# Samples' x and small vectors on SyncE's queue, the next columns' first weight steps inside the opening's list, and that list in another order

## The chip, the cores and the metric

The kernel runs on one core of a Trainium2 chip. A core has five engines with a queue of instructions each, which run side by side and wait for one another through semaphores: TensorE (PE, matmuls; its weight loads are shown apart as PEld), VectorE (DVE), ScalarE (ACT), GpSimd (POOL) and SyncE (SP, which here only issues DMAs). ACT and POOL can issue DMAs too. Such an issue takes its place in the engine's queue: what stands behind it waits until it has been issued. The metric is the time of one execution in microseconds (us); less is better.

## The reference

One step of a decoder layer, with a prompt of 1024 rows and 8 samples of 8 rows (1088 rows in all), 1024 columns wide:

```
shift, scale, gate = silu(c) @ w_ada + b_ada
h = rmsnorm(x, norm_g) * (1 + scale) + shift
u_pool | z_pool | z_ssm | xBC | dt | g = h @ w_in
p = (pool_mix(u_pool) * silu(z_pool)) @ w_pool_out
s = rmsnorm((SSD(silu(conv(xBC))) + D*x) * silu(z_ssm)) @ w_ssm_out
x = x + gate * ((sigmoid(g_pool) * p + sigmoid(g_ssm) * s) @ w_o);   y = rmsnorm(x, final_g)
```

c has one row for the prompt and one for each sample, so that the modulation (shift, scale, gate) is a table of 9 rows. The states of pooling, convolution and SSD are outputs too.

## The kernel before

Everything is f32; a matmul operand is cut into a high part (rounded to the fast format, by ACT) and a low part (the rest, by DVE or POOL), and a product is three matmuls: high by high, low by high, high by low. The big projection h @ w_in is done two columns of 128 at a time, with one level of Strassen (seven half-size products for eight): a "pair". A pair loads its two columns into two tiles named rawA (three buffers in all), whose halves are b11, b21, b12, b22; from them come t3 = b22 - b12, t2 = t3 + b11, t4 = t2 - b21 and b12 - b11 (line 368), and each of the seven is split (lines 153 and 156). On the other side stand sums of parts of h, kept as S1 to S4.

The kernel has an opening (function first, lines 641 to 1087), then a long stage of pairs (products at line 414), the SSD and the output products. The change touches the opening and what follows it at once.

The opening does its work by a list, ORDER1 (line 611): each word is a small function for one or a few instructions, and each engine, SP among them, runs its part of the words in the order of the list (in_line). A letter behind a word says the engine: V for DVE, A for ACT, G for POOL. The words:

- sq (line 667 on DVE, 669 on ACT) squares a tile of x and sums it. Tiles 0 to 7 are the prompt's, 128 rows each; tile 8 is the samples'. root, unit, spread and rsb (lines 673 to 703) turn the sums of a group of tiles into a row factor, spread over the partitions. The groups are tiles 0 and 1, 2 to 4, and 5 to 8.
- turn (709) transposes one column block k of one group on PE; out (714) multiplies it by the row factor into tf.
- silu, tab, cturn, sct (718 to 729) prepare c; vturn, vt (732 to 736) the small vectors vb. ada (759) multiplies c by one eighth of a quarter of w_ada; mr, end, md (764 to 779) turn a quarter's result into columns and add the biases. So md0 to md3 give shift and scale for two column blocks each.
- h, ta, t, l (790 to 812) apply the modulation and split h. hi, lo, pr (825 to 842) are the split and the products of the first two gate columns, sg their sigmoid (853).
- dt, dto, gt, ge (864 to 884) make dt and the gate's table; ge also stores the table (884). lx, lt, lc are the late small vectors.
- ca, cb, cc, ce (918 to 927) are the Strassen sums of h, s1h to s4h and s1l to s4l (931, 933 and 654) their splits; tc, tb, d21, d12, wh, wl (line 825 and 654) the weights of the opening's own pair, m (982) its products, u and z (998 to 1010, 991) what is made of them.
- warm runs matmuls of ones.

A word that subtracts or adds on DVE or POOL does so in a helper at line 654, so many rows have that line.

DMAs of the opening: ACT issues c (lines 133, 134), the samples' x (139) and four small loads into vb (141 to 144), ahead of all its other work. SP works through a list `waiting`, each entry as soon as the words it names have been said:

```
for what in ("x07", "p0", "w", "p1", "p2"):
waiting += [((), lambda: w_load(0, 1)), (("lo0.0",), lambda: w_load(1, 1))]
waiting += [(("ada1.6",), lambda k=k: ada_load(3, k)) for k in range(KT)]
waiting += [((), lambda: dtw.append(dt_w()))]
waiting += [(("end1",) + tuple(f"sq{i}" for i in range(9)), lambda: col(0)), (("end2",), lambda: col(1))]
waiting += [((), lambda: late.append(late_loads())), ((), bg_load)]
waiting += [(tuple(f"turn2.{k}" for k in range(KT)), lambda k=k: gate_load(k)) for k in range(KT)]
```

That is eight tiles of x, the first quarter of w_ada, the first halves of two gate columns, two quarters of w_ada, the other halves, the last quarter, dt's weights, the opening's own two columns (948), the late small vectors (251 to 255), the gate's bias (1028) and the gate's third of w_ada (609).

The pairs after the opening are run by run_units, which fetches the weights of a pair (pair_w, line 351) one unit ahead: it loads the columns, splits b11, and leaves the other steps in a generator (steps), of which the pair before does some between its products and the pair itself the rest. The first of these pairs (columns 2 and 3 of z) is built after the opening; but its instructions aren't in the list, and the scheduler of the program may put them between the list's instructions where it thinks an engine free.

## Time and profile before

| | us |
|---|---|
| median of 3 runs (1271.11 to 1277.57) | 1273.59 |
| profiled execution, as it was timed | 1276.04 |
| its span in the profile | 1274.3 |
| PE busy in the span | 1245.2 (98%) |
| DVE, ACT, POOL busy | 976.5, 682.1, 729.6 |
| first product of the pair after the opening starts | 106.32 |

A row of a timeline has the start and the length in us, the engine, the line, the operation, what it writes and reads, the shapes, how many instructions are put together in it, and in brackets how long the engine had been idle and what ended that. Rows of an engine with a q (ACTq, SPq) are DMA issues: their time is that of the issue, not of the transfer. A row of busy time by stretch has its columns told where it is shown.

### The profile page before, as it was taken

How to read it: one execution, taken by the hardware profiler on the slowest of the kernel's cores; microseconds unless marked ns; L12 is line 12 of the kernel's file. 1: busy time of each engine (PE TensorE's matmuls, PEld its weight loads, DVE VectorE, ACT ScalarE, POOL GpSimd, SP SyncE). 2: the span in 40 equal slices, each digit the busy share in tenths (PEclk: the TensorE clock that was granted, in tenths of full speed). 3: DMA queues.
4: the chain of work that ended last, by engine and by line, in shares of the span. 5: the costliest groups of instructions: out<-in, count | busy, mean ns of one | idle time of the engine just before them, and what ended most of it. 6: DMA issues, size and time to landing. Idle time of an engine off the chain costs nothing.

```text
span 1274.3 us, 26561 instructions
## 1 busy us (share of the span) xinstructions
PE 1245.2 (98%) x9733; PEld 1163.7 (91%) x9733; DVE 976.5 (77%) x1709; ACT 682.1 (54%) x1568; POOL 729.6 (57%) x617
## 2 busy tenths in 40 slices
...
GB/s 323 297 97 192 139 156 153 183 190 158 166 162 196 162 154 169 139 147 120 184 167 196 162 182 155 318 314 269 249 237 282 272 256 244 276 214 222 248 194 154
DMA packets 264676, 258.00 MB, mean 202 GB/s; under 512 B 29889, under 2 KB 204561, under 8 KB 264538
## 3 DMA queue, kind: packets, MB, share of 16 engines
...
## 4 chain that ended last, share of the span: by engine, by line
PE 86%; DVE 4%; DMA 4%; ACT 3%; issue 2%; POOL 1%; SPq 1%; ACTq 0%; POOLq 0%; DVEq 0%
PE ps L414 22%; PE mm L414 22%; PE mm L239 16%; PE pc L414 5%; PE ps L1256 2%; PE pc L1578 2%; PE ps L2060 2%; PE ps L2062 2%; PE ps L2061 2%; PE ps L1259 2%; DMA R<-in_w_o 1%; PE ps L1346 1%; PE ps L1553 1%; PE ps L982 1%; DMA wo<-R 1%
## 5 line engine op out<-in xcount | busy, mean ns | idle before, releaser
L156 POOL TENSOR_TENSOR wlo<-rawA,whi 128x512 fp32r<-128x512 f32 x120 | 174.7, 1460 | 110.6 <-ACT whi L153 98.5
L156 POOL TENSOR_TENSOR wlo<-raw,whi 128x512 fp32r<-128x512 f32 x90 | 149.2, 1665 | 86.3 <-ACT whi L153 74.3
L239 PE MATMUL mm<-Y,whi 128*128 128x352 f32 (+1 forms) x960 | 197.5, 336 | 0.5 <-ACT G L1787 0.3
L239 PEld LDWEIGHTS mm<-Y,whi 128*128 128x128 f32 x960 | 160.4, 190 | 7.1 <-issue 4.8
L1099 DVE SCALAR_TENSOR_TENSOR GA<-GA,cvT,GA 128x1112 f32<-128x1112 f32 x72 | 131.2, 1826 | 0.1
L414 PE MATMUL mm<-Y,whi 128*128 128x272 f32 x800 | 120.2, 292 | 0.0
L153 ACT ACTIVATE whi<-rawA 128x512 fp32r<-128x512 f32 x120 | 75.3, 627 | 82.8 <-PE ps L414 45.1
L414 PE MATMUL ps<-Y,whi 128*128 128x272 f32 x800 | 117.8, 290 | 0.0
L153 ACT ACTIVATE whi<-raw 128x512 fp32r<-128x512 f32 x90 | 56.0, 629 | 110.1 <-DVE raw L368 50.7
L414 PEld LDWEIGHTS mm<-Y,whi 128*128 128x128 f32 x800 | 107.9, 188 | 2.7 <-issue 0.9
L414 PEld LDWEIGHTS ps<-Y,whi 128*128 128x128 f32 x800 | 106.7, 188 | 0.4
L1244 ACT ACTIVATE dec<-dec,acT 128x128 f32<-128x128 f32 (+1 forms) x288 | 87.0, 383 | 30.2 <-POOL dec L1235 28.7
L239 PE MATMUL mm<-Y,wlo 128*128 128x352 f32 (+1 forms) x480 | 99.3, 329 | 0.0
L239 PEld LDWEIGHTS mm<-Y,wlo 128*128 128x128 f32 x480 | 82.2, 189 | 0.0
L306 POOL TENSOR_TENSOR pw<-pw,ph 128x512 fp32r<-128x512 f32 x40 | 69.8, 1745 | 11.9 <-ACT ph L304 11.7
L414 PE MATMUL mm<-G,whi 128*128 128x272 f32 x480 | 71.1, 290 | 0.0
L414 PE MATMUL ps<-G,whi 128*128 128x272 f32 x480 | 70.3, 289 | 0.0
L414 PE MATMUL mm<-Y,wlo 128*128 128x272 f32 x400 | 66.7, 289 | 0.0
L414 PE MATMUL ps<-Y,wlo 128*128 128x272 f32 x400 | 66.6, 288 | 0.0
L414 PEld LDWEIGHTS mm<-G,whi 128*128 128x128 f32 x480 | 64.5, 189 | 0.7
L414 PEld LDWEIGHTS ps<-G,whi 128*128 128x128 f32 x480 | 64.2, 188 | 0.0
L1515 POOL TENSOR_TENSOR Y<-xb,Y 128x512 fp32r<-128x512 f32 x32 | 41.6, 1301 | 36.1 <-ACT Y L1513 36.1
...
## 6 DMA issues: line engine op xcount, KB each, us to landing
...
```

Source lines behind the costliest of these rows:

```text
L153: ins = act(hi[:, :, :ncols], raw[:, :, :ncols], AF.Copy)
L156: (eng or nc.gpsimd).tensor_tensor(lo[:, :, :ncols], raw[:, :, :ncols], hi[:, :, :ncols].bitcast(F32), ALU.subtract)
L239: mm(ps[:, :n], w[k // 4][h][:, k % 4, :], r[k][:, o:o + n], start=(j == 0), stop=(j == len(terms) - 1))
L306: nc.gpsimd.tensor_tensor(raw.bitcast(F32R), raw, hi.bitcast(F32), ALU.subtract)
L414: mm(p, w[j // 8][:, k], A(k, s)[j // 4 == 1], start=(j == 0), stop=(j == 11))
L1099: V.scalar_tensor_tensor(d[:, :n], rp[:, k:k + n], cvT[:, 24 * k + mc:24 * k + mc + 1], d[:, :n], ALU.mult, ALU.add)
L1244: act(dec[:, h], dec[:, h], AF.Exp, bias=acT[:S, c, 8 * g + h:8 * g + h + 1], scale=-1.0)
L1256: mm(o[hh], xd[:S, 2 * q + hh, :], dec[:S, 2 * q + hh], start=True, stop=state is None)
L1259: mm(o[hh], state[:, h * 64:h * 64 + 64], cE[:, h], start=False, stop=True)
L1515: nc.gpsimd.tensor_tensor(yl[g][:, :, o:o + S], v, yhc.bitcast(F32), ALU.subtract)
L1578: mm(pu, bt, xw.rearrange("p h d -> p (h d)"), start=True, stop=True)
L2060: mm(ps, hi, y[:, k, c0:c0 + cw], start=(first and k == 0), stop=False)
```

## The change

Three things. The samples' x and the four small vectors are no longer issued by ACT; SP issues them, the vectors between the second and the third tile of x, the samples between the fifth and the sixth. The first pair after the opening is fetched inside the list (word nw: its two loads and the split of b11), and so are the split of b21 (n1), t3 and t2 (nt3, nt2), the split of t2 (n2) and b12 - b11 (nd); the rest of its preparation follows the list. And the list is in another order, with the engine of some words changed; the gate's third of w_ada is loaded ahead of the late vectors and the gate's bias.

```diff
@@ -136,12 +136,7 @@
     act(rc[:, 0:1], eps, AF.Silu)
     nc.gpsimd.memset(rc[:, 0:1], 1.0)
     xs_ = R([P, D])
-    store_(xs_[:NS], x_sample.rearrange("b t d -> (b t) d"))
     vb = sm.tile([44, P], F32, tag="stc", name="vb", bufs=4)
-    store_(vb[0:16, :], b_ada[0, 0:2048].rearrange("(m p) -> m p", p=P))
-    store_(vb[16:24, :], norm_g[0].rearrange("(m p) -> m p", p=P))
-    store_(vb[24:40, :], ssm_norm_g[0].rearrange("(m p) -> m p", p=P))
-    store_(vb[40:44, :], pool_scale[0].rearrange("(m p) -> m p", p=P))
     scT = const([P, KT, 32], "scT")
     nc.gpsimd.memset(scT, 0.0)
     vT = const([P, 44], "vT")
@@ -348,7 +343,7 @@
 
     highs = []
 
-    def pair_w(c0, c1, pri, second):
+    def pair_w(c0, c1, pri, second, apart=False):
         def run():
             with tc.high_priority(pri):
                 cols = []
@@ -396,11 +391,28 @@
                 add(t2)
                 add(b22)
                 yield
+            def apart_():
+                t3, t2 = raw_(), raw_()
+                fine["n1"] = lambda: add(b21)
+                fine["nt3"] = lambda: diff(t3, b22, b12)
+                fine["nt2"] = lambda: diff(t2, t3, b11, ALU.add)
+                fine["n2"] = lambda: add(t2)
+                fine["nd"] = lambda: diff(b12, b12, b11)
+
+                def rest():
+                    t4 = raw_()
+                    add(t3)
+                    diff(t4, t2, b21, eng=nc.gpsimd)
+                    add(b12)
+                    add(t4)
+                    add(b22)
+                    yield
+                return rest()
             add(b11)
-            prep_q.append(steps())
+            prep_q.append(apart_() if apart else steps())
             return w, prep_q[-1]
         return run
-    prep_q = []
+    prep_q, fine = [], {}
 
     turn, banks_ = [0], [(PB, PA)]
 
@@ -453,7 +465,7 @@
         yield
         product(w[5], s4_part, out(d1, 0, u2, u2))
 
-    def pair(c0, c1, f0, f1, pri=PRI, second=True):
+    def pair(c0, c1, f0, f1, pri=PRI, second=True, apart=False):
         def run(w):
             w, prep = w
             prep_q.remove(prep)
@@ -468,7 +480,7 @@
             for it in its:
                 next(it, None)
             later.extend(its)
-        get_w = pair_w(c0, c1, pri, second)
+        get_w = pair_w(c0, c1, pri, second, apart)
 
         def ws():
             w = get_w()
@@ -609,28 +621,28 @@
         load(gw[k], w_ada[0, k * P:(k + 1) * P, 2 * D:])
 
     ORDER1 = """
-        warm6 sq0.V silu sq1.V turn0.7 tab turn0.5 turn0.3 cturn turn0.2 root0 turn0.6 turn0.0 unit0.V warm2
-        sct sq8.A spread0 warm3 rsb0.A sq2.A vturn out0.7 turn0.1 warm6 sq3.V out0.1 sq4.A vt turn1.4 out0.5
-        turn1.5 out0.2 turn1.2 root1 sq5.V turn1.7 unit1.A warm4 out0.6 out0.3 spread1 out0.0 turn1.0 sq7.V
-        rsb1.A turn2.7 sq6.A turn2.6 warm1 out1.2 ada0.0 out1.4 root2 unit2.A turn2.0 out1.0 turn2.5 out1.5
-        turn2.3 out1.7 spread2 turn2.4 rsb2.A ada0.2 out2.7 ada0.4 out2.0 ada0.6 out2.3 mr0 turn2.2 out2.4
-        hi0.0 end0 out2.2 turn2.1 lo0.0.G hi1.0 turn1.6 md0 turn1.3 turn0.4 turn1.1 lo1.0.V h0.0 ada1.0 h1.0
-        ta2.0.V warm3 out1.1 t1.0.A t2.0 h1.1 ada1.2 t0.0.V warm4 h0.1 l1.0.G out2.1 h2.0 out1.6 ta2.1.A
-        ada1.4 l2.0.V t0.1.A pr1.0 t2.1 t1.1.A l0.1.G out1.3 h2.1 ada1.6 out0.4 mr1 pr2.0 l2.1.V l0.0.V
-        l1.1.G out2.5 end1 out2.6 pr2.1 md1 pr0.0 ta2.2.V ta2.3.A t2.2 pr1.1 h1.2 t2.3 h0.3 pr0.1 h2.2
-        t0.3.V h2.3 ada2.0 l2.2.V h0.2 ada2.2 l2.3.V hi0.1 ada2.4 t0.2.V h1.3 lo0.1.V ada2.6 hi1.1 t1.3.V
-        pr2.2 mr2 l0.2.V t1.2.A lo1.1.V end2 l1.3.V pr2.3 l0.3.G md2 ta2.5.V pr0.2 h1.4 ta2.4.V t1.4.A t2.5
-        ada3.0 h0.4 ada3.2 t2.4 h1.5 ada3.4 t0.4.V t1.5.A ada3.6 l1.2.V h2.4 pr0.3 l1.5.V mr3 l2.4.V pr1.2
-        h2.5 h0.5 l0.4.V l1.4.V end3 t0.5.A pr0.4 l0.5.V pr1.3 l2.5.G md3 pr0.5 h0.7 tc.V t0.7.A pr2.4 h1.7
-        l0.7.V wh0 ca1.V pr1.4 h0.6 tb.V h1.6 t0.6.V pr2.5 s1h1 l0.6.V wh1 s1l1.V pr0.6 t1.6.A lx pr1.5
-        t1.7.A l1.6.V ta2.6.A wl0.V pr0.7 l1.7.V ta2.7.A m0.0 d12.V sgt t2.7 pr1.6 wl1.V sg0.0 t2.6 u0.0
-        m0.1 sg0.1 ca0.V h2.6 d21.V s1h0 lt l2.6.V m1.0 u0.1 s1l0.V h2.7 wh4 l2.7.V pr2.6 wl4.V ca2.V m1.1
-        ca3.V s1h2 cb2.V s1h3 cc2.V pr2.7 wh5 ce2.V s1l3.V pr1.7 sg2.1 cb3.G lc sg2.0 gt0 dt2 s1l2.V sg1.1
-        cc3.V wh2 ce3.V sg1.0 wl2.V wh3 cb0.V gt2 dto2 wl3.V dt0 cc0.V s2h2 s2h0 s2l2.V gt4 dto0 s2l0.V dt1
-        cb1.G u1.0 s2h3 u1.1 z1.0 z1.1 cc1.V gt6 s2l3.V s4h3 m2.0 ge s3h2 s4l3.V s3h3 s3l2.V s2h1 m2.1
-        s3l3.V s3h0 s2l1.V s3h1 dto1 s3l1.V m3.0 s3l0.V s4h2 ce1.V u2.0 u2.1 s4l2.V m3.1 s4h1 u3.0 wh6
-        s4l1.V ce0.G m4.0 u3.1 wl5.G s4h0 m4.1 u4.0 s4l0.V wl6.G m5.0 u4.1 m5.1 u5.0 z5.0 m6.0 u5.1 z5.1
-        m6.1 u6.0 u6.1
+        silu warm4 sq0.V tab cturn sq1.V turn0.7 turn0.6 turn0.4 sct turn0.2 root0 turn0.0 unit0.A vturn
+        turn0.5 vt warm1 sq2.A spread0 sq3.V warm3 rsb0.A turn0.1 out0.0 sq4.A out0.4 turn1.0 out0.2 turn1.5
+        out0.7 turn1.1 root1 out0.5 turn1.6 unit1.V turn1.2 warm3 out0.1 sq5.A out0.6 turn1.7 spread1 warm2
+        sq6.V rsb1.A sq8.A turn1.3 warm6 sq7.V out1.7 root2 ada0.0 out1.1 unit2.A turn2.3 out1.2 turn2.7
+        out1.6 turn2.2 out1.5 spread2 out1.3 out1.0 turn2.6 rsb2.A turn2.0 turn1.4 out2.2 turn0.3 out2.0
+        turn2.4 out2.7 turn2.5 out2.4 hi0.0 ada0.2 out1.4 lo0.0.G ada0.4 hi1.0 out2.3 ada0.6 out2.5 mr0
+        turn2.1 lo1.0.V end0 out2.6 ada1.0 md0 warm1 ada1.2 ta2.0.V h1.0 warm4 out2.1 h0.1 t2.0 h1.1 ada1.4
+        warm4 h0.0 ta2.1.V t1.0.V h2.0 t2.1 t1.1.A ada1.6 warm1 mr1 t0.0.V h2.1 l1.1.V end1 t0.1.A l2.0.V
+        ada2.0 l0.0.G md1 pr2.0 l2.1.V ta2.2.A ta2.3.V pr0.0 h0.2 t2.2 pr2.1 h1.2 t2.3 h1.3 h2.2 ada2.2 h2.3
+        l2.2.V ada2.4 t1.2.A l0.1.V ada2.6 l2.3.V hi0.1 pr2.2 mr2 l1.2.V hi1.1 lo0.1.V t0.2.A end2 lo1.1.V
+        pr2.3 l0.2.V l1.0.G md2 pr0.1 out0.3 h0.4 ta2.4.V pr1.0 h0.3 ta2.5.V h1.5 t0.4.V pr0.2 t2.5 t1.5.A
+        pr1.1 l0.4.V h2.5 l1.5.V h1.4 pr1.2 h0.5 t1.4.V t0.5.A l2.5.V ada3.0 t0.3.A t2.4 ada3.2 l0.3.G
+        ada3.4 h2.4 ada3.6 ca1.V mr3 pr0.3 l2.4.V s1h1 l0.5.V end3 t1.3.A pr2.4 cb1.V s1l1.V l1.4.G md3
+        pr0.4 pr2.5 l1.3.V h1.6 ca0.V h1.7 pr0.5 tc.V h0.6 pr1.3 cc1.V t0.6.A cb0.V h0.7 pr1.4 t0.7.A l0.6.V
+        cc0.V wh1 pr0.6 l0.7.V wh0 s1h0 pr1.5 wl0.V t1.6.A d12.V pr0.7 t1.7.A s1l0.V m0.0 ce0.V sgt l1.6.V
+        l1.7.V pr1.6 sg0.0 ta2.6.V tb.V u0.0 m0.1 sg0.1 t2.6 ta2.7.A wl1.V h2.6 pr1.7 d21.V u0.1 wh4 l2.6.V
+        m1.0 sg1.1 t2.7 sg1.0 wl4.V pr2.6 ca2.V h2.7 s1h2 l2.7.V m1.1 ca3.V cb2.V s1h3 pr2.7 cc2.V wh5 lx
+        wl5.G gt0 wh2 dt2 sg2.0 cb3.V sg2.1 cc3.V wl2.V wh3 ce3.V wl3.V gt2 dto2 dt1 ce2.V s1l3.V s2h3 s2h0
+        s2l3.V s2h1 s2l0.G s2h2 u1.0 gt4 u1.1 s4h2 dt0 s2l1.G z1.0 z1.1 gt6 s4l2.V dto1 m2.0 ge s2l2.V s3h0
+        s3h2 s3l0.G lt s3h3 m2.1 lc u2.0 s3h1 s3l2.V s4h0 s3l3.V m3.0 u2.1 s4l0.V wh6 dto0 s3l1.V wl6.G m3.1
+        s4h3 u3.0 s1l2.G m4.0 nw u3.1 m4.1 u4.0 ce1.V s4l3.G s4h1 m5.0 u4.1 n1 s4l1.V m5.1 u5.0 nt3 z5.0
+        m6.0 u5.1 m6.1 u6.0 z5.1 nt2 n2 u6.1 nd
     """.split()
 
     def first():
@@ -1027,9 +1039,26 @@
             for j in range(4):
                 load(bg[32 * j:32 * j + NB + 1], b_ada[0, 2 * D + 256 * j:2 * D + 256 * j + 256].partition_broadcast(NB + 1))
 
+        ahead = []
+
+        def nw():
+            assert not waiting
+            ahead.append(light[1][0]())
+            light[1] = (lambda: ahead[0], light[1][1])
+
+        def vb_load():
+            load(vb[0:16, :], b_ada[0, 0:2048].rearrange("(m p) -> m p", p=P))
+            load(vb[16:24, :], norm_g[0].rearrange("(m p) -> m p", p=P))
+            load(vb[24:40, :], ssm_norm_g[0].rearrange("(m p) -> m p", p=P))
+            load(vb[40:44, :], pool_scale[0].rearrange("(m p) -> m p", p=P))
+
         waiting = []
-        for what in ("x07", "p0", "w", "p1", "p2"):
-            if what == "w":
+        for what in ("x01", "vb", "x24", "smp", "x57", "p0", "w", "p1", "p2"):
+            if what == "vb":
+                waiting += [((), vb_load)]
+            elif what == "smp":
+                waiting += [((), lambda: load(xr[8][0][:NS], x_sample.rearrange("b t d -> (b t) d")))]
+            elif what == "w":
                 waiting += [((), lambda t=t: w_load(t, 0)) for t in range(2)]
             elif what[0] == "x":
                 waiting += [((), lambda i=i: x_load(i)) for i in range(int(what[1]), int(what[2]) + 1)]
@@ -1039,8 +1068,8 @@
         waiting += [(("ada1.6",), lambda k=k: ada_load(3, k)) for k in range(KT)]
         waiting += [((), lambda: dtw.append(dt_w()))]
         waiting += [(("end1",) + tuple(f"sq{i}" for i in range(9)), lambda: col(0)), (("end2",), lambda: col(1))]
+        waiting += [(tuple(f"turn2.{k}" for k in range(KT)), lambda k=k: gate_load(k)) for k in range(KT)]
         waiting += [((), lambda: late.append(late_loads())), ((), bg_load)]
-        waiting += [(tuple(f"turn2.{k}" for k in range(KT)), lambda k=k: gate_load(k)) for k in range(KT)]
 
         def loads():
             while waiting and said.issuperset(waiting[0][0]):
@@ -1051,6 +1080,9 @@
                      hi=hi, lo=lo, pr=pr, sgt=lambda: None, sg=sg, dt=dt, dto=dto, gt=gt, ge=ge, lx=lx, lt=lt, lc=lc,
                      ca=ca, cb=cb, cc=cc, ce=ce, d21=d21, d12=d12, wh=wh, wl=wl, m=m, u=u, z=zz)
         calls.update(tb=t2, tc=t3)
+        calls["nw"] = nw
+        for name in ("n1", "nt3", "nt2", "n2", "nd"):
+            calls[name] = lambda name=name: fine[name]()
         for n in range(1, 5):
             calls[f"s{n}h"] = lambda *a, n=n: sh(f"s{n}", *a)
             calls[f"s{n}l"] = lambda *a, n=n: sl(f"s{n}", *a)
@@ -1485,7 +1517,7 @@
         return pair(C_UP + gi * P, C_ZP + gi * P, u_unit(gi), zp_unit(gi), second=False)
 
     def gpair(c0, func, d, second=False):
-        return pair(c0, c0 + P, to_dram(func, d[0]), to_dram(func, d[1]), PRI, second)
+        return pair(c0, c0 + P, to_dram(func, d[0]), to_dram(func, d[1]), PRI, second, second)
 
     zpairs = [gpair(C_Z + m * P, AF.Silu, (z_d[m // 4][:, m % 4], z_d[m // 4][:, m % 4 + 1]), m == 2) for m in range(0, 16, 2)]
     gpairs = [gpair(C_G + m * P, AF.Sigmoid, gp_d[m:m + 2]) for m in range(0, 8, 2)]
```

## The prediction

> **What bounds the kernel now.** I read the page first, then busy time by stretch, the timelines of the engines in the first 110 us, and the chain of waits there. The change touches the opening: everything up to the first product of the column pair that follows the list.
>
> ```profile
> span 1274.3 us, 26561 instructions
> ```
> ```profile
> 0.00:15.50 15.50, 9.10 (x42) 8.12 (x43) 3.26 (x8) 5.51 (x9) 2.39 (x31) 1.00 0.89 302
> 15.50:31.70 16.20, 16.20 (x165) 13.34 (x163) 12.56 (x31) 8.50 (x21) 1.27 (x1) 1.00 1.11 342
> 31.70:54.20 22.50, 21.74 (x282) 18.40 (x281) 19.98 (x52) 16.82 (x32) 5.20 (x5) 1.00 0.98 284
> 54.20:83.40 29.20, 28.70 (x275) 21.65 (x273) 24.61 (x42) 20.65 (x36) 6.77 (x4) 1.00 0.55 196
> 83.40:106.30 22.90, 18.23 (x124) 17.79 (x121) 17.14 (x29) 11.87 (x25) 8.44 (x7) 0.85 0.27 84
> 106.30:640.00 533.70, 532.81 (x4224) 523.73 (x4223) 421.15 (x663) 296.60 (x677) 375.50 (x247) 1.00 0.52 164
> 90.00:95.00 5.00, 2.78 (x12) 2.78 (x13) 5.00 (x10) 2.60 (x7) 0.00 (x0) 0.62 0.14 47
> 95.00:100.00 5.00, 5.00 (x31) 5.00 (x30) 2.12 (x5) 1.46 (x3) 2.75 (x2) 0.69 0.55 159
> ```
>
> The columns are the stretch, its length, busy time of PE, weight loads, DVE, ACT and POOL, the granted TensorE clock, the DMA share and GB/s. From 106.3 to 640 PE is busy 532.81 of 533.70 us: that stage runs at PE's pace, so what the opening gains or loses arrives at the end one for one. In the opening PE is short of work in two places, the first 15.5 us and 83.4 to 106.3. In between it is filled, DVE almost as much.
>
> The first place, on ACT and then on DVE:
>
> ```profile
> 1.40 0.30 ACTq L134 DMA_DIRECT2D R<-in_c_sample  x1
> 4.96 0.32 ACTq L143 DMA_DIRECT2D vb<-in_ssm_norm_g  x1
> 9.70 0.25 ACTq L144 DMA_DIRECT2D vb<-in_pool_scale  x1
> 10.00 1.05 ACT L718 ACTIVATE R<-R 9x1024 f32<-9x1024 f32 x1 [6.77 <-DMA R<-in_x_sample]
> 15.35 0.38 ACT L701 ACTIVATE rsb<-mm 128x256 f32<-128x256 f32 x1 [1.35 <-PE mm L692]
> ```
> ```profile
> 6.08 1.23 DVE L667 SCALAR_TENSOR_TENSOR sqj<-Y 128x1024 f32<-128x1024 f32 x1 [0.26 <-DMA Y<-in_x_prompt]
> 15.76 0.42 DVE L714 TENSOR_TENSOR tf<-ps,rsb 128x256 f32<-128x256 f32 x1 [1.95 <-ACT rsb L701]
> ```
>
> ACT's silu (L718) doesn't use the samples' x. It stands behind ACT's own DMA issues, and the last of these (pool_scale) can't be issued before x_sample has landed. The first two tiles of x were squared by 7.3, yet their first product out comes at 15.76.
>
> The second place, on PE, DVE and POOL:
>
> ```profile
> 88.97 0.77 PE L982 MATMUL ps<-Y,whi 128*128 128x272 f32 x4 [2.19 <-ACT Y L933]
> 92.22 1.05 PE L982 MATMUL ps<-Y,whi 128*128 128x272 f32 x3 [2.48 <-DVE Y L654]
> 98.81 1.16 PE L982 MATMUL ps<-Y,whi 128*128 128x272 f32 x8
> 100.32 0.55 PE L982 MATMUL ps<-R,whi 128*128 128x272 f32 x3
> 106.32 0.92 PE L414 MATMUL ps<-Y,whi 128*128 128x272 f32 x6
> ```
> ```profile
> 84.36 0.69 DVE L368 TENSOR_TENSOR raw<-rawA 128x512 f32<-128x512 f32 x1 [1.81 <-DMA rawA<-in_w_in]
> 86.90 0.69 DVE L368 TENSOR_TENSOR rawA<-rawA,rawA 128x512 f32<-128x512 f32 x1
> 87.50 1.79 DVE L654 TENSOR_TENSOR Y<-tf,Y 128x544 fp32r<-128x544 f32 x1
> 89.22 0.41 DVE L882 TENSOR_TENSOR bg<-pc,bg 128x256 f32<-128x256 f32 x1
> 94.00 0.71 DVE L654 TENSOR_TENSOR Y<-tf,Y 128x544 fp32r<-128x544 f32 x1
> ```
> ```profile
> 87.12 1.59 POOL L368 TENSOR_TENSOR raw<-raw,rawA 128x512 f32<-128x512 f32 x1 [3.43 <-DVE raw L368]
> ```
>
> The next pair's three differences (L368, first and last shown) are not in the list, but the scheduler has put them into DVE's queue in the middle of it, and the first waits 1.81 us for its column. PE then waits 2.19 and 2.48 us for the parts behind them, and the granted clock falls: 0.62 and 0.69 over ten us, a loss of 5 x 0.38 + 5 x 0.31 = 3.4 us. This place costs 2.19 + 2.48 + 3.4 = 8.1 us. (88.97 and 92.22 follow the holes; one product takes 100.32 - 98.81 = 1.5.)
>
> **The change, part by part.**
>
> Five issues leave ACT's queue (x_sample and four vectors). Silu then waits for c_sample alone, 32 KB issued at 1.40. x1, 512 KB issued about then, had landed when DVE squared it at 6.08; the landing of c_sample lies between, and I take 5.0. From silu to the spread of the first group is 15.35 - 10.00 = 5.35 us before; the scaled diagonal moves from DVE to ACT there, and one square on ACT still stands between. So 10.35, and the first product out at 10.8 instead of 15.76: 5.0 us.
>
> The same five go into SP's queue, four between x1 and x2, one between x4 and x5, ahead of all weights.
>
> ```profile
> 6.08 0.33 SPq L186 DMA_DIRECT2D Y<-in_x_prompt  x1
> 9.46 0.33 SPq L186 DMA_DIRECT2D Y<-in_x_prompt  x1
> ```
>
> The sixth and seventh tiles of x are issued only at 6.08 and 9.46, as earlier loads land, so the number of loads under way is limited, and four small ones take places of large ones. Four issues at 0.25 to 0.32 us (ACT's rows) move x2's by 1.2. That costs nothing while x0 and x1 still transfer, till x1's landing before 6.08; without that cover it costs 1.2. Bytes are the same. All loads up to the last part of the modulation weights are 13.9 MB (x 4.2, samples 0.3, four parts 8.4, four column halves 1.0): 302 x 15.5 us and 342 x 16.2 us give 10.2 MB by 31.7, the other 3.7 MB at 284 GB/s land at 44.7. No stage below is forecast ahead of that.
>
> The list itself has the same work. Fifteen of its steps change between DVE and ACT, the others between DVE and POOL. What the first group gains, the next keep as long as DVE can follow:
>
> ```profile
> L714 DVE TENSOR_TENSOR tf<-ps,rsb 128x384 f32<-128x384 f32 x6 | 3.3, 544 | 0.0
> L714 DVE TENSOR_TENSOR tf<-ps,rsb 128x448 f32<-128x448 f32 x4 | 2.4, 616 | 2.9 <-ACT rsb L701 2.9
> L714 DVE TENSOR_TENSOR tf<-ps,rsb 128x256 f32<-128x256 f32 x5 | 2.0, 417 | 2.0 <-ACT rsb L701 2.0
> ```
> ```profile
> 31.53 0.16 DVE L774 TENSOR_TENSOR md<-ps,vT 128x18 f32<-128x18 f32 x1
> 54.28 0.17 DVE L774 TENSOR_TENSOR md<-mm,vT 128x18 f32<-128x18 f32 x1
> ```
>
> From 10.8 to the first modulation (md0) DVE has seven 0.42, eight 0.55, seven 0.61, two squares of 1.3, and 1.7 of small ones: 15.9 us, so md0 at 26.7 against 31.7. From md0 to md3 before: 22.8. Products out with 2.9 us of DVE have moved ahead of md0, three sums and parts of 0.71 have moved in: 22.0. So md3 at 48.7 against 54.45: 5.8 us.
>
> From md3 to the pair: 106.32 - 54.45 = 51.9 us, less the 8.1 of the second place: 43.8 of PE work. The L368 steps go behind the last products, where PE has 3 us per split: DVE is free of 1.81 + 3 x 0.69 = 3.9 us. Against that five parts go from DVE to POOL and three back; with wl5, wl6 and the next columns' splits some four more POOL operations than before stand ahead of the last part needed. A DVE operation beside one took 1.79 instead of 0.71: 4 x 1.08 = 4.3. So DVE has about what it had, from an earlier start, and its late parts meet PE's need closely; I keep 3 us for waits there. 48.7 + 43.8 + 3 = 95.5.
>
> Weight steps inside the list: two loads on SP behind the four stores of the gate, three splits on ACT and POOL, three DVE steps.
>
> ```profile
> 75.14 3.54 SPq L357 DMA_DIRECT2D rawA<-in_w_in  x2
> 89.66 1.37 SPq L884 DMA_DIRECT2D gate_d<-bg  x4
> ```
>
> They come later than before (75.14): after the gate's sum, the stores take 1.4 us. A column took from its issue in the second half of that 3.54 us row (till 78.7) to DVE's 84.36, about 6; a lone one less. What is queued behind: on ACT the split of the first column waits for it, and S4's second high part and the last silus stand behind; on POOL one S4 low part. The last gate product is followed by m2 to m5, eight products of 1.5, before m6 needs them: 12 us, against 0.4 + 1.4 + 6 + 0.7 + 1.6 + 1.6 = 11.7 for the gate's sum, its stores, the load, ACT's high part (as long as DVE's 0.69), and two low parts on POOL (as long as its difference, 1.59). So nothing if the gate's sum follows its last product at once, and up to 3 if it is as late as before; I put it within the 3 kept. The rest of that pair's preparation, before done by 88.7, now follows the list: four splits and a POOL difference of 1.59, hidden behind products of 1.5 us, twice each; without that cover 1.6.
>
> The gate's eight loads go ahead of four small ones and the bias. The bias is used in the gate's sum (before at 89.22), the small ones by steps among the last products: nothing, unless those loads came 30 us late.
>
> The warm-up matmuls are 29 as before, elsewhere.
>
> ```profile
> 13.39 1.06 PE L749 MATMUL pc<-ones 128*128 128x128 f32 x4
> 16.83 1.50 PE L749 MATMUL pc<-ones 128*128 128x128 f32 x12
> 18.17 0.49 PE L709 MATMUL ps<-ident,Y 128*128 128x128 f32 x3
> ```
>
> Four took 1.06 us there; twelve, later, 18.17 - 16.83 = 1.34, 0.11 each. So PE was at half pace at first, and at full pace within 5.7 us of its start at 11.1 (silu's end). In the new order it starts at about 6.1, and full pace at 11.8 is early enough. [...]
>
> **Sum.** 106.3 to 95.5 is -10.8. The profiled execution has a span of 1274.3 and took 1276.04; so 1265.2. That execution lay 2.45 over the median of 1273.59, so 1262.8 as a median.
>
> **Rivals.**
>
> A, the forecast: 1262.8.
>
> B: the front comes 5.8 earlier, but DVE and POOL are late again at the S parts, and the hole and the clock's fall stay. For it: the 1.79 us beside POOL, and more POOL steps. Against: 3.9 us taken from DVE. 1273.6 - 5.8 = 1267.8.
>
> C: the small loads hold x back, so that silu's 5 us aren't used; only the second place gains, 8.1 - 3 = 5: 1268.5. For it: the issues at 6.08 and 9.46. Against: DMA share 0.89 over the first 15.5 us.
>
> D, slower: PE stays at half pace up to md0, because its first stretch is now cut by waits for x and banks. PE's 16.20 busy us of 15.5 to 31.7 would become up to 32.4, 16 more: -10.8 + 16 = +5, so 1279. It decides once half pace lasts 11 us of PE's work beyond 11.8, to about 34. Against it: warm words stand at all those waits. [...] The trace speaks against it as far as it goes: three transposes at 18.17 took 0.49 where four matmuls of ones had taken 1.06, though they stood right behind such matmuls.
>
> E: nothing, what is won is given back in the pair stage: 1273.6.
>
> **How the numbers follow.** A 0.54, B 0.17, C 0.08, D 0.14, E 0.07. A difference under 0.5% (6.4 us: 1267.2 to 1280.0) can't be told from none. Faster: 0.51 of A, 0.06 of B, 0.03 of C: 0.60. Slower: 0.11 of D, 0.02 of E: 0.13. Same: 0.27. A alone runs from 1257 (no waits kept, md3 close to the 44.7 that the loads allow) to 1267. The range, 1257 to 1276, leaves out most of D and a little of A.
>
> **What would show it.** Silu on ACT at about 5; first product out at about 11; the last md line at about 49; no L368 on DVE before the last products; the first L414 product at about 95; the granted clock 1.00 from 90 to 100. It would be wrong if L714 starts after 13, if four matmuls of ones still take about 1 us after 20, if PE waits over 3 us before m6 for the split column, or if the stretch after the opening lasts longer than 534 us to the same product.

## The result, and the profile after

The changed kernel takes 1264.78 us (median of 9 runs, 1259.61 to 1270.67), the kernel before 1273.59 us (9 runs). The ratio is 0.9938, with a 95% interval of 0.9914 to 0.9961. The profiled execution took 1264.58 us, and its page says:

```profile
span 1262.9 us, 26588 instructions
```

So the span fell by 11.4 us. The two places of the opening first. ACT's and DVE's timelines of the changed kernel (line numbers moved: silu 730, spread to rsb 713, product out 726, modulation 786, differences 363):

```profile
5.28 1.05 ACT L730 ACTIVATE R<-R 9x1024 f32<-9x1024 f32 x1 [2.06 <-DMA R<-in_c_sample]
11.94 0.38 ACT L713 ACTIVATE rsb<-ps 128x256 f32<-128x256 f32 x1 [1.75 <-PE ps L704]
59.31 0.38 ACT L865 ACTIVATE g<-ps 128x256 f32<-128x256 f32 x1
61.38 0.40 ACTq L866 DMA_DIRECT2D gs<-g  x1
63.48 0.40 ACT L1010 ACTIVATE s<-mm 128x272 f32<-128x272 f32 x1 [3.79 <-DMA gs<-g]
```
```profile
12.36 0.76 DVE L726 TENSOR_TENSOR tf<-mm,rsb 128x256 f32<-128x256 f32 x2 [0.77 <-ACT rsb L713]
16.27 1.23 DVE L679 SCALAR_TENSOR_TENSOR sqj<-Y 128x1024 f32<-128x1024 f32 x1 [0.53 <-DMA Y<-in_x_prompt]
23.65 0.62 DVE L726 TENSOR_TENSOR tf<-ps,rsb 128x448 f32<-128x448 f32 x1 [1.41 <-ACT rsb L713]
29.16 0.17 DVE L786 TENSOR_TENSOR md<-ps,vT 128x18 f32<-128x18 f32 x1
51.43 0.17 DVE L786 TENSOR_TENSOR md<-mm,vT 128x18 f32<-128x18 f32 x1
94.90 0.68 DVE L363 TENSOR_TENSOR raw<-rawA 128x512 f32<-128x512 f32 x1
98.86 1.64 DVE L363 TENSOR_TENSOR rawA<-rawA,rawA 128x512 f32<-128x512 f32 x1
```

Silu came 4.7 us earlier, the first product out 3.4 (12.36 for 15.76), md0 2.4 (29.33 for 31.69, the ends of those rows), md3 2.85 (51.60 for 54.45). The three differences of the next columns now stand among the last products (94.90 to 98.86), and the hole is gone. PE of the changed kernel at the same places, and behind them one row of the kernel before:

```profile
8.26 0.64 PE L721 MATMUL mm<-ident,Y 128*128 128x128 f32 x2
8.68 0.63 PE L721 MATMUL ps<-ident,Y 128*128 128x128 f32 x2
10.85 1.06 PE L704 MATMUL ps<-R,ones 128*128 128x128 f32 x4
63.93 1.28 PE L994 MATMUL mm<-G,whi 128*128 128x272 f32 x8 [0.70 <-ACT s L1010]
69.61 0.47 PE L852 MATMUL mm<-G,whi 128*128 128x448 f32 x1 [0.80 <-ACT G L804]
97.74 0.92 PE L426 MATMUL ps<-Y,whi 128*128 128x272 f32 x6
100.52 1.17 PE L426 MATMUL ps<-G,whi 128*128 128x272 f32 x8
```
```profile
109.36 1.18 PE L414 MATMUL ps<-G,whi 128*128 128x272 f32 x8
```

The pair's first product starts at 97.74 (two of its matmuls had slipped in at 95.12) for 106.32. Since its first matmuls mix with the list's last ones, kernels are compared below by the row that follows the first 24 matmuls, the pair's second product: 109.36 before, 100.52 after, 8.8 us earlier. Between 51.60 and 100 PE waits twice, 0.70 and 0.80, both on ACT. Busy time by stretch (stretch, length, busy PE, weight loads, DVE, ACT, POOL, granted clock, DMA share, GB/s):

```profile
60.00:70.00 10.00, 8.40 (x54) 7.54 (x54) 5.07 (x12) 4.54 (x10) 0.00 (x0) 1.00 0.30 96
90.00:95.00 5.00, 5.00 (x43) 5.00 (x42) 4.51 (x8) 1.61 (x3) 4.56 (x3) 1.00 0.71 199
95.00:100.00 5.00, 5.00 (x42) 5.00 (x41) 5.00 (x8) 2.14 (x5) 2.59 (x2) 1.00 0.25 91
```

From 90 to 100 PE is full at clock 1.00, where it had 0.62 and 0.69. The stretch that lost time is now 60 to 70. A first reading: of silu's 4.7 us only 2.85 arrived at md3, part of that was then lost again to a wait of ACT for a store (3.79 at 63.48), and the hole of the S parts is gone, be it through the steps in the list or through the list's order.

### The profile page after: what moved, and what is told of

Read it like the earlier page. It is cut to its first block, busy times and chain, and to the rows that moved or that the text cites. A ratio compares the mean times of both kernels' runs of the same rounds, so it can differ in the third digit from the quotient of the medians.

```text
span 1262.9 us, 26588 instructions
## 1 busy us (share of the span) xinstructions
PE 1241.1 (98%) x9747; PEld 1159.9 (92%) x9747; DVE 977.8 (77%) x1709; ACT 680.7 (54%) x1567; POOL 728.5 (58%) x618
## 4 chain that ended last, share of the span: by engine, by line
PE 61%; DMA 5%; DVE 3%; issue 1%; ACT 1%; POOL 1%; SPq 0%; ACTq 0%; DVEq 0%
PE mm L234 16%; PE mm L426 13%; PE ps L426 13%; PE ps L1288 2%; PE pc L426 2%; PE pc L1610 2%; PE ps L2092 2%; PE ps L2094 2%; PE ps L1291 2%; PE ps L2093 2%; DMA dec<-acs_d 1%; PE ps L1378 1%; PE ps L1585 1%; PE ps L1401 1%; DMA Y<-yp 1%
```

## The experiments

The theory (1): the front gains because ACT's queue is free of five issues, the second place because the weight steps left DVE's queue. The rivals: the new order carries the gain; small loads hold x back; PE's half pace holds the front; the gain of the front is lost again before the pair. All runs in one table; times in us from each kernel's profiled execution, the "clock" is the mean granted clock of the span, the ratio is to the kernel before, with its interval. What the expectations call the pair's 24th product is the row of the pair's second product. Each trace is one execution: a_late has the changed kernel's front and yet its md3 is 1.2 us earlier, so a difference of about 1 us between two traces decides nothing by itself.

| kernel | silu | md3 ends | pair's 2nd product | span | clock | ratio |
|---|---|---|---|---|---|---|
| before | 10.00 | 54.45 | 109.36 | 1274.3 | 0.994 | |
| after | 5.28 | 51.60 | 100.52 | 1262.9 | 0.998 | 0.9938 (0.9914 to 0.9961) |
| a_act: small loads on ACT again | 9.65 | 55.25 | 101.79 | 1263.5 | 0.999 | 0.9952 (0.9934 to 0.9969) |
| a_nonw: weight steps not in the list | 4.63 | 51.60 | 100.89 | 1266.0 | 0.995 | 0.9947 (0.9927 to 0.9966) |
| a_order: both undone | 9.59 | 55.17 | 104.27 | 1272.9 | 0.993 | 0.9988 (0.9965 to 1.001) |
| b_queue: before, small loads on SP | 5.12 | 51.48 | 106.99 | 1271.9 | 0.995 | 0.9996 (0.9978 to 1.0014) |
| b_nw: before, weight steps in the list | 9.68 | 54.42 | 103.63 | 1268.5 | 0.995 | 0.9964 (0.9949 to 0.9979) |
| a_late | 4.82 | 50.42 | 99.67 | 1260.5 | 0.998 | 0.9943 (0.9922 to 0.9964) |
| a_warm12 | 4.78 | 52.74 | 99.94 | 1261.1 | 0.996 | 0.9925 (0.9904 to 0.9946) |
| a_xfirst | 4.74 | 52.14 | 99.70 | 1261.4 | 0.998 | 0.9919 (0.9900 to 0.9938) |
| a_split | 5.18 | 50.25 | 99.14 | 1259.3 | 0.998 | 0.9946 (0.9924 to 0.9967) |
| a_buf | 4.98 | 51.75 | 98.95 | 1260.6 | 0.998 | 0.9918 (0.9893 to 0.9943) |
| a_best | 5.21 | 51.09 | 99.24 | 1260.7 | 0.995 | 0.9920 (0.9901 to 0.9938) |
| a_last | 4.91 | 52.05 | 97.93 | 1260.9 | 0.997 | 0.9911 (0.9887 to 0.9935) |

**The parts, one undone or one alone.** First a_act, which gives the five issues back to ACT:

```diff
+    store_(xs_[:NS], x_sample.rearrange("b t d -> (b t) d"))
+    store_(vb[0:16, :], b_ada[0, 0:2048].rearrange("(m p) -> m p", p=P))
...
-        for what in ("x01", "vb", "x24", "smp", "x57", "p0", "w", "p1", "p2"):
+        for what in ("x07", "p0", "w", "p1", "p2"):
```

> The changed kernel with one part undone: the samples' x and the four small vectors are issued by ScalarE again, at the old place; list and weight steps stay. Theory 1 (the forecast's): the front gain comes from ScalarE's queue, so silu goes back to about 10, the first product out to about 16 and md3 from 51.6 to 54 or later; the pair's first products move from 97.4 to about 100, the time is 3 to 5 us over the changed kernel (ratio to the kernel before 0.996 to 0.998). Theory 2: the new order of the list carries the front gain; silu goes back to 10 but md3 stays below 52.5 and the ratio at 0.994. Theory 3: the small loads within x's tiles cost more than they bring; x's tiles land earlier, and md3 comes before 51.

Silu went to 9.65 and md3 to 55.25, so the front's gain is ACT's queue, as theory 1 had it: 3.65 us at md3. (With the new list and these loads on ACT, in a_act and a_order, md3 is even 0.7 to 0.8 later than in the kernel before.) But the pair came only 1.27 later. ACT's timeline of this kernel shows where the rest went:

```profile
63.38 0.37 ACTq L871 DMA_DIRECT2D gs<-g  x1
65.19 0.40 ACT L1015 ACTIVATE s<-mm 128x272 f32<-128x272 f32 x1 [1.85 <-DMA gs<-g]
```

Here the store of g lands 1.8 after its issue, and PE has no wait at all between md3 and the pair. In the changed kernel the same instruction waits 3.79. The copy of the first product (L1010) writes the tile s1, in which the first sigmoid g had stood, so it waits until the store of g has landed; md3 is earlier by 3.65, this copy only by 1.7. b_queue is the same part alone, in the old list:

```diff
-        for what in ("x07", "p0", "w", "p1", "p2"):
+        for what in ("x01", "vb", "x24", "smp", "x57", "p0", "w", "p1", "p2"):
-        sct sq8.A spread0 ... rsb1.A turn2.7
+        sct spread0 ... rsb1.A sq8.A turn2.7
```

> The kernel before with one part alone: the samples' x and the small vectors within x's tiles on SyncE; in the old list only the square of the samples' tile moves, behind the second group's row factor, since its tile now lands later. Theory 1: silu at 5.3, first product out at 11 to 12.5, md3 at 51 to 52 instead of 54.4, and 2 to 3 us of that arrive at the pair (103.5), ratio 0.997 to 0.999. Theory 2: the old order waits elsewhere (PE's order, x's tiles) and md3 stays at 54: ratio 1.000.

md3 gained 2.97, as expected, and none of it passed this store. The copy in the kernel before, then ACT and PE of b_queue:

```profile
64.94 0.40 ACT L998 ACTIVATE s<-mm 128x272 f32<-128x272 f32 x1 [1.84 <-PE ps L982]
```
```profile
60.16 0.37 ACTq L848 DMA_DIRECT2D gs<-g  x1
65.39 0.40 ACT L992 ACTIVATE s<-mm 128x272 f32<-128x272 f32 x1 [5.26 <-DMA gs<-g]
```
```profile
65.84 0.46 PE L887 MATMUL mm<-ident,va 120*128 120x120 f32 x1 [3.88 <-ACT s L992]
90.02 0.77 PE L976 MATMUL ps<-Y,whi 128*128 128x272 f32 x4 [0.53 <-ACT Y L927]
92.46 0.64 PE L976 MATMUL ps<-Y,whi 128*128 128x272 f32 x3 [1.67 <-DVE Y L648]
```
```profile
64.00:70.00 6.00, 4.16 (x16) 3.87 (x17) 2.87 (x5) 3.07 (x7) 0.00 (x0) 0.52 0.11 37
85.00:95.00 10.00, 7.80 (x69) 6.64 (x62) 10.00 (x17) 7.78 (x15) 1.62 (x1) 1.00 0.15 52
```

The copy started at 65.39; in the kernel before it had been 64.94. In the stretch of that hole of 3.88 us the clock fell as well, to 0.52 from 64 to 70. What b_queue gained at the pair (2.4, the number of theory 1) came from elsewhere: the two holes of the second place are smaller (0.53 and 1.67 us for 2.19 and 2.48), and between 85 and 95 the clock stayed at 1.00 (before: 0.81).

Now the weight steps. a_nonw takes the words nw, n1, nt3, nt2, n2, nd out of the new list; the scheduler then places them:

```diff
-        s1l2.G m4.0 nw u3.1 m4.1 u4.0 ce1.V s4l3.G s4h1 m5.0 u4.1 n1 s4l1.V m5.1 u5.0 nt3 z5.0 ...
+        s1l2.G m4.0 u3.1 m4.1 u4.0 ce1.V s4l3.G s4h1 m5.0 u4.1 s4l1.V m5.1 u5.0 z5.0 ...
-    return pair(..., PRI, second, second)
+    return pair(..., PRI, second)
```

> The changed kernel with one part undone: the next columns' first weight steps are not in the list, the scheduler places them (the three differences then stand in VectorE's queue ahead of most last products, the splits of b11 and b21 in ScalarE's ahead of a high part). Theory 1: VectorE and ScalarE wait there for the columns, PE gets holes of 2 us and more behind late parts, the granted clock falls below 0.9 in some five us between 80 and 97, and the pair's first products come at 100 to 103 instead of 97.4: ratio 0.996 to 0.999. Theory 2: with the new order the columns are loaded early enough and nothing waits; 97 to 98, ratio 0.994, the hole of the kernel before was the old order's.

The pair is 0.37 later, nearly theory 2. But there is a hole, by another engine: in ACT's queue the split of the first column of the pair after this one stands ahead of one of the last high parts (L943) and waits 5.42 for its load, and PE waits behind that part.

```profile
93.79 0.63 ACT L148 ACTIVATE whi<-rawA 128x512 fp32r<-128x512 f32 x1 [5.42 <-DMA rawA<-in_w_in]
94.33 0.64 ACT L943 ACTIVATE Y<-tf 128x544 fp32r<-128x544 f32 x1
```
```profile
95.02 0.76 PE L994 MATMUL ps<-Y,whi 128*128 128x272 f32 x4 [1.34 <-ACT Y L943]
```

It costs 1.6 by the rows of PE (this kernel was 1.23 ahead of the changed one at the 69.61 row and 0.40 behind it at 95.02), masked by a store of g that happened to be issued and to land 0.5 earlier, by which PE's wait of 0.80 went too. b_nw is the same part alone, in the old list:

```diff
-        s4l1.V ce0.G m4.0 u3.1 wl5.G s4h0 m4.1 u4.0 s4l0.V wl6.G m5.0 u4.1 m5.1 u5.0 z5.0 m6.0 u5.1 z5.1
-        m6.1 u6.0 u6.1
+        s4l1.V ce0.G m4.0 nw u3.1 wl5.G s4h0 m4.1 u4.0 s4l0.V wl6.G m5.0 u4.1 n1 m5.1 u5.0 nt3 z5.0 m6.0 u5.1 z5.1
+        nt2 n2 m6.1 u6.0 u6.1 nd
```

> The kernel before with one part alone: the next columns' first weight steps as words of the old list, at its end as in the changed kernel. Theory 1: md3 stays at 54.4, the differences leave VectorE's queue, the holes of 2.2 and 2.5 us and the clock's fall go: first products of the pair at 98 to 101 instead of 106.3, ratio 0.994 to 0.996. Theory 2: the old order is late by itself (parts beside GpSimd), the hole stays: 105 to 107, ratio 0.999 to 1.001.

The pair came at 103.63, 5.7 us earlier: the two holes of 2.19 and 2.48 shrank to 0.28 and 0.26, and the clock is 1.00.

```profile
87.70 0.76 PE L999 MATMUL ps<-Y,whi 128*128 128x272 f32 x4 [0.28 <-ACT Y L950]
88.72 0.65 PE L999 MATMUL ps<-Y,whi 128*128 128x272 f32 x3 [0.26 <-DVE Y L671]
```

a_order undoes both parts, so that the new list is left (with the order of SP's last loads):

> The changed kernel with both other parts undone (small loads on ScalarE, the next columns' steps left to the scheduler): the new order of the list and the order of SyncE's last loads are all that is left of the change. Theory 1, parts that replace each other: undoing either alone cost only 0.4 and 1.3 us at the pair's products, since the new order already keeps VectorE's late parts out of the hole; then this kernel keeps 6 to 8 of the 8.8 us (the 24th product of the pair at 101.5 to 103.5, before 109.36, changed kernel 100.52), ratio 0.993 to 0.996. Theory 2, either part is enough to remove the hole but one is needed: 105 or later, ratio 0.997 to 1.000.

The list alone brings the pair to 104.27, 5.1 of the 8.8 us, less than theory 1 had; PE waits 1.61 there for a high part that stands behind such a split on ACT. So the parts replace each other: the weight steps are worth 5.7 in the old list, 2.5 in the new one with a late front (a_order against a_act), 0.4 with an early one. The 0.4 is within what two traces differ by. None of them alone makes the result.

**The store's wait.** Two things can hold that copy: the issue itself (59.7 when g is ready, 61.38 when it goes), and the landing. a_late puts SP's small late loads ahead of the gate's eight loads of 512 KB again (4 MB; the expectations say 2):

```diff
-        waiting += [(tuple(f"turn2.{k}" ...), lambda k=k: gate_load(k)) for k in range(KT)]
         waiting += [((), lambda: late.append(late_loads())), ((), bg_load)]
+        waiting += [(tuple(f"turn2.{k}" ...), lambda k=k: gate_load(k)) for k in range(KT)]
```

> The changed kernel with only the order of SyncE's last entries undone: late small vectors and bias ahead of the gate's third of the modulation weights, as before the change. Theory 1: ScalarE's first store of g (issued 61.38) waited for a semaphore that the load of conv_w held, which stood behind the gate's 2 MB; with the small loads in front the store goes at 59.7, the copy of the first product at 61.7 to 62 instead of 63.48, PE's waits of 0.8 and 0.7 shrink, and the 24th product of the pair comes 1 to 2 us earlier (98.5 to 99.5); ratio 0.992 to 0.993. Theory 2: the store waits for the transfers as such, since the DMA engines are full to 59: same times as the changed kernel. Rival: the gate's loads are now late for the gate's products and the pair comes later.

The issue went at once (58.54, 0.03 us after g), but the store then took 3.7 us to land; the copy waited 3.77 instead of 3.79. That the gate's loads were still running is the author's estimate from the kernel before, where SP has them in the same order: it issues them from 49.32 to 54.74, and the DMA share there is 0.99 from 60 to 61, 0.89 from 61 to 62 and 0.07 from 62 to 63.

```profile
58.54 0.37 ACTq L866 DMA_DIRECT2D gs<-g  x1
62.28 0.40 ACT L1010 ACTIVATE s<-mm 128x272 f32<-128x272 f32 x1 [3.77 <-DMA gs<-g]
```

Theory 2 holds for this step; the 0.85 us at the pair came from a front that was 1.2 earlier in this execution. a_buf takes the other one away: the first block's two sigmoids share the tile u3, which is written later, so the copy into s1 waits for no store.

```diff
-                buf = pa.tile([P, HF], F32, tag=("s1", "u2", "u3", "c2")[2 * b + t], name=nm("g0"))
+                tag = "u3" if b == 0 else ("u2", "c2")[t]
+                if tag not in narrow:
+                    narrow[tag] = pa.tile([P, HF], F32, tag=tag, name=nm("g0"))
+                buf = narrow[tag][:, 256 * t:] if b == 0 else narrow[tag]
```

> The changed kernel with one thing else: the first block's sigmoids lie together in the tile u3, so that the copy of the first product (tile s1) no longer waits until the first store of g has landed. Theory 1: ScalarE idled 3.79 there (59.7 to 63.5) since the store landed only when the load stream had drained; without it the copy runs at about 60, PE's waits of 0.7 and 0.8 behind it go, and the pair's 24th product comes 1.2 to 1.8 earlier than 100.52. Theory 2: the next store's semaphore or the next tile holds ScalarE instead; less than 0.5.

```profile
61.48 0.40 ACTq L869 DMA_DIRECT2D gs<-g  x1
61.92 0.40 ACT L1013 ACTIVATE s<-mm 128x272 f32<-128x272 f32 x1 [2.08 <-DMA va<-in_conv_w]
```

The pair came 1.57 earlier, as expected, and what is left of the wait has its cause in the row: the issue on ACT's queue, 1.6 us after g was ready, waited until SP's load of conv_w had landed (61.41 in the chain of waits), which stood behind the gate's loads. (The ratio, 0.9918, has an interval that overlaps with that of the changed kernel.) a_last, below, has both taken away.

**The front.** a_warm12 lets PE work from 1.1 on:

```diff
-        silu warm4 sq0.V tab ...
+        silu warm12 sq0.V tab ...
```

> The changed kernel with 12 instead of 4 matmuls of ones at the start (PE then works from 1.1 to about 6 instead of 3.1, before anything it needs is there). Theory 1: PE's half pace up to 12.6 made the spread late; with full pace by about 5 the row factor rsb0 starts at 10.3 to 10.8 instead of 11.94, the first product out at 10.8 to 11.2, md3 1 us earlier, the pair at most 1 us earlier. Theory 2: x's tiles and the small vectors' landing (vturn at 9.68) set rsb0; it moves by less than 0.4. Theory 3 (transposes don't keep the full pace): the transposes from 7.4 on still take 0.63 a pair, as before.

PE and busy time by stretch of a_warm12:

```profile
7.52 0.38 PE L721 MATMUL mm<-ident,Y 128*128 128x128 f32 x2
7.74 0.38 PE L721 MATMUL ps<-ident,Y 128*128 128x128 f32 x2
12.91 0.93 PE L721 MATMUL mm<-ident,Y 128*128 128x128 f32 x4 [1.13 <-DMA Y<-in_x_prompt]
```
```profile
10.00:13.00 3.00, 1.04 (x8) 0.56 (x7) 2.61 (x7) 0.12 (x2) 0.00 (x0) 1.00 1.06 202
13.00:16.00 3.00, 3.00 (x16) 3.00 (x17) 1.52 (x6) 2.01 (x4) 0.00 (x0) 0.53 0.98 371
```

Transpositions follow each other in 0.22 a pair instead of 0.42, the row factor rsb0 comes at 9.63 instead of 11.94. Silu was 0.5 earlier in this execution; from silu to rsb0 it is 4.85 us instead of 6.66, and PE's half pace was what held it. But then PE waits 0.83 us for a product out on DVE and 1.13 for a tile of x, does only 1.04 us of work from 10 to 13, the granted clock falls to 0.53, and md3 is 1.1 later than in the changed kernel, not 1 us earlier. (The pair came 0.6 earlier all the same.) As soon as PE isn't late, the front waits for x's tiles; part of md3's delay may be the loads of this execution, 299 GB/s from 7 to 10 us for 345.

a_xfirst puts the small loads behind all of x:

```diff
-        for what in ("x01", "vb", "x24", "smp", "x57", "p0", "w", "p1", "p2"):
+        for what in ("x07", "vb", "smp", "p0", "w", "p1", "p2"):
-        turn0.0 unit0.A vturn turn0.5 vt ... out2.2 turn0.3
+        turn0.0 unit0.A turn0.5 ... out2.2 vturn vt turn0.3
```

> The changed kernel with the small vectors and the samples' x behind all eight tiles of x on SyncE (the small vectors' transpose moves in the list to just ahead of the first gate column's split). Theory 1: the slow stretch of 213 GB/s at 10 to 13 us comes from the samples' tile (64 rows); it moves to the samples' transfer behind x, x's tiles 4 to 7 land 1 to 2 us earlier, and the waits for x of 0.34, 0.85, 0.53 and 0.18 go; rsb0 at 11 to 11.5 since PE loses the transposition ahead of the spread; md0 0.5 to 1.5 earlier. Theory 2: the stretch belongs to that time or to x's own rows; it stays at 9 to 13 with x alone under way, and nothing moves by more than 0.5.

Busy time by stretch, of the changed kernel and of a_xfirst:

```profile
10.00:13.00 3.00, 3.00 (x18) 2.94 (x18) 2.15 (x6) 0.91 (x4) 0.00 (x0) 1.00 1.00 213
13.00:16.00 3.00, 2.92 (x26) 2.62 (x25) 2.63 (x10) 2.12 (x5) 0.00 (x0) 1.00 1.00 381
```
```profile
10.00:13.00 3.00, 2.98 (x25) 2.66 (x24) 1.82 (x6) 2.21 (x5) 0.00 (x0) 1.00 1.04 408
13.00:16.00 3.00, 2.87 (x25) 2.55 (x23) 2.96 (x9) 1.13 (x4) 0.00 (x0) 1.00 1.06 270
```

The slow stretch moved with the samples' load, from 10 to 13 us (213 GB/s, DMA engines busy all the time) to 13 to 16 (270). No engine waits for x any more from 10 us on (in the changed kernel DVE 0.7 and ACT 1.2), and the third group's row factor came at 21.73 instead of 23.07. md0 didn't follow (29.87): the small vectors' copy now stood on DVE ahead of six products out and took 2.2 us with its wait. The pair came 0.8 earlier, with md3 0.5 later: here the first store of g was issued as soon as g was ready, at 60.26.

a_split asks why the samples' load is slow. Their 64 rows go to partitions 0 to 31 and 64 to 95:

```diff
-    xr = {8: (xs_, NS)}
+    xr = {8: (xs_, 96)}
+    HALVES = ((0, 0), (32, 64))
-                waiting += [((), lambda: load(xr[8][0][:NS], x_sample.rearrange("b t d -> (b t) d")))]
+                waiting += [((), lambda r=r, p=p: load(xs_[p:p + 32], x_sample.rearrange("b t d -> (b t) d")[r:r + 32])) for r, p in HALVES]
```

> The changed kernel with one thing else: the samples' 64 rows of x lie on partitions 0 to 31 and 64 to 95 instead of 0 to 63 (two loads of 32 rows at the same place of SyncE's queue; rows 32 to 63 are zero, PE picks the 64 columns with the identity's columns, ScalarE squares 96 rows). Theory 1: the slow stretch at 10 to 13 us (213 GB/s with the DMA engines 1.00 busy) is the samples' load, which writes to half of SBUF's partitions only; spread over both halves it goes at the rate around it, 350 GB/s or more in all three-us windows from 7 to 16, 4.5 MB are moved by 14.5 instead of 16.0, x's last tiles land 1 to 1.5 earlier and md0 and md3 come 0.5 to 1.5 earlier. Theory 2: it is the length of the load or the place in memory; the stretch stays at 200 to 280 GB/s. [...]

The stretch of a_split, then the same of a_late, whose front is that of the changed kernel:

```profile
10.00:13.00 3.00, 2.98 (x20) 2.73 (x21) 2.37 (x7) 1.42 (x5) 0.00 (x0) 1.00 0.99 311
```
```profile
10.00:13.00 3.00, 2.98 (x26) 2.69 (x26) 2.80 (x8) 1.72 (x4) 0.00 (x0) 1.00 0.93 317
```

311 GB/s would have been half a proof, but a_late reached 317 without the edit, and its md3 was as early (50.42, a_split 50.25). The better test is a_best, in which the divided load stands behind x. It has the edits of a_xfirst, a_split and a_buf, and moves three words:

```diff
-        out1.2 turn2.7 out1.6 turn2.2 out1.5 spread2 out1.3 out1.0 turn2.6
+        out1.2 spread2 turn2.7 out1.6 turn2.2 out1.5 vturn out1.3 out1.0 vt turn2.6
```

> A version out of what helped: the changed kernel with small vectors and samples behind x (1 us at the pair's products by its trace), the samples on both halves of the partitions, the first block's sigmoids in u3, the small vectors' transpose where VectorE idles, and the third group's spread two transposes earlier on PE (VectorE idled 2.3 before that group's row factor). If these add up: row factor of the third group at 20 to 21 instead of 23.07, md0 at 27 to 28, md3 at 49 to 50.5, the pair's 24th product at 97.5 to 99, ratio to the kernel before 0.989 to 0.991. If PE's work from md3 on or the load stream bounds the opening: 99 to 100, ratio 0.992.

```profile
13.00:16.00 3.00, 2.97 (x26) 2.63 (x23) 2.96 (x10) 1.14 (x4) 0.00 (x0) 1.00 1.03 218
```

The stretch behind x is slow again, 218 GB/s (undivided 270 in a_xfirst and 212 in a_last, below), so dividing doesn't cure it. The front gained (rsb2 at 20.14, md0 at 28.06), but the pair, at 99.24, is later than expected and no better than in a_buf: its first store of g was issued at 62.47, 3.3 us after g was ready, with SP's load of conv_w again behind the gate's.

Last, a_last: the edits of a_buf, a_late and a_xfirst (the samples undivided), and a_best's move of words:

```diff
-        for what in ("x01", "vb", "x24", "smp", "x57", "p0", "w", "p1", "p2"):
+        for what in ("x07", "vb", "smp", "p0", "w", "p1", "p2"):
-        waiting += [(tuple(f"turn2.{k}" ...), lambda k=k: gate_load(k)) for k in range(KT)]
         waiting += [((), lambda: late.append(late_loads())), ((), bg_load)]
+        waiting += [(tuple(f"turn2.{k}" ...), lambda k=k: gate_load(k)) for k in range(KT)]
-                buf = pa.tile([P, HF], F32, tag=("s1", "u2", "u3", "c2")[2 * b + t], name=nm("g0"))
+                buf = narrow[tag][:, 256 * t:] if b == 0 else narrow[tag]
```

> The changed kernel with small vectors and samples (undivided, on partitions 0 to 63) behind x, the first block's sigmoids in u3, the late small vectors and the bias ahead of the gate's loads, the small vectors' transpose where VectorE idles and the third group's spread two transposes earlier. Theory 1: the two waits of ScalarE at the first store of g are in series (a semaphore that a small load behind the gate's 2 MB holds, then the store's landing); the tile alone took off 1.6 at the pair, with both gone PE has no wait after md3 (46.5 us to the pair's 24th product, as where ScalarE issued the small loads), and with md3 at 50 to 51 that product comes at 96.5 to 97.5: ratio to the kernel before 0.989 to 0.991. Theory 2: PE's work from md0 on, without waits, is what is left and md3 stays at 51 or later, since the modulation's weights now end the wait: 98 to 99, ratio 0.992. The slow stretch of the loads follows the samples' load to 13 to 16 us in both.

```profile
60.16 0.37 ACTq L869 DMA_DIRECT2D gs<-g  x1
60.58 0.40 ACT L1013 ACTIVATE s<-ps 128x272 f32<-128x272 f32 x1 [0.45 <-ACT g L868]
```

The store goes at once, the copy follows it at once, and PE has no wait between md3 and the pair: 45.9 us from 52.05 to 97.93, against 48.9 in the changed kernel. Of these 3.0 us 1.6 are idle time of PE that is gone; the other 1.4 are work that PE had done before the later md3. With md3 at 52.05 the time lies between the two theories. It is the best version at the pair (2.6 us ahead of the changed kernel) and by its median, 1262.82 us (6 runs), though a_buf's, 1263.04, can't be told from that. That it beats the kernel before is measured; against the changed kernel the intervals of the ratios overlap.

## Why the prediction was right, point by point

The time, 1264.8, is 2 us over the predicted 1262.8, and rival A, the forecast, is what happened in its mechanism: silu left the queue of ACT's loads, and the second place went. Its terms were less good than their sum.

- **Silu at 5.0**: 5.28, right; a_act shows that it was ACT's queue. **rsb0 at 10.35**: 11.94. The step that failed is "full pace at 11.8 is early enough": PE's half pace lasted until about 12.6 (a pair of transpositions took 0.42 at 8.26 and 0.22 at 12.63), and the spread stood in PE's queue behind six transpositions, the small vectors' one and a matmul of ones at that pace. From silu to rsb0 it took 6.66 us for 5.35; a_warm12, at full pace, took 4.85.
- **md0 at 26.7, md3 at 48.7**: 29.33 and 51.60. The front's term was mis-sized, 2.85 for 5.8: 1.6 us of the difference were lost up to the first product out, 1.1 from there to md0, 0.3 to md3. From the first product out to md0 DVE worked 14.5 us, 1.4 less than the sum of the forecast, but waited 2.5, of which 0.7 for x and 1.4 for the third group's row factor. "That costs nothing while x0 and x1 still transfer" was wrong for the samples' load: with it between x4 and x5 the last tiles of x came later (a_xfirst). (Of the steps that change between DVE and ACT the prediction counts fifteen; they are fourteen, and the sum doesn't use the count.)
- **md0 to md3 22.0**: 22.3. **md3 to the pair 46.8**, 3 of them for waits: 46.1, with 1.5 us of waits in the named rows. They weren't where they were kept for (late parts, the split column), but at a store of g, so that the total fits is luck. "The gate's eight loads go ahead of four small ones: nothing" missed it: one of the small ones held the issue of that store until it had landed (a_buf's row), and with the 4 MB behind the small ones the store landed 3.7 us after its issue (a_late; that the 4 MB held it there is an estimate).
- **The second place goes**: right, the clock is 1.00 and no part is late. That it goes because of the steps in the list is only half the cause; a_order and b_nw show that the order and the steps replace each other, and the forecast had given the order nothing there.
- **The pair at 95.5**: 97.74, so -8.6 instead of -10.8. **One for one behind it**: the span gained 11.4, that is 2.8 more. Part of it is the clock in the long stages. Rows of the kernel before, of the changed kernel and of a_order:

```profile
1115.00:1135.00 20.00, 20.00 (x122) 19.97 (x121) 6.22 (x19) 0.41 (x2) 0.00 (x0) 0.91 0.59 201
```
```profile
1115.00:1135.00 20.00, 20.00 (x132) 19.68 (x131) 12.79 (x31) 0.57 (x3) 0.60 (x2) 1.00 0.78 274
```
```profile
1115.00:1135.00 20.00, 20.00 (x123) 19.97 (x122) 7.04 (x20) 0.41 (x2) 0.00 (x0) 0.91 0.58 203
```

  A clock of 0.91 over 20 us is a loss of 1.8 us. Added up in stretches of ten us from 100 on, the clock cost the kernel before 2.2 us, the changed kernel 0.5 and a_order 7.0; from the pair's second product to the end the kernels took between 1160.2 (a_split) and 1168.6 us (a_order), with the lowest mean clock in the longest. The same kernel varies as much: the changed kernel's nine runs go from 1257.9 us at a mean clock of 0.998 to 1269.0 at 0.993. So in the profiled executions the two errors, 2.2 too much up to the pair and 2.8 too little behind it, cancelled; of the second 1.7 are the clock's, by the nine runs mostly chance, and the rest stays open. In the medians the first error stands, 8.8 us for 10.8, and that fits the pair's 8.6 to 8.8 better than the span's 11.4 does.
- **Rivals**: B (the hole stays) and E fell at once. C named the right place, SP's order within x, though not the size. D fell, though half pace did hold the first row factor: in a_warm12 transpositions behind matmuls of ones went at 0.22 a pair from 7.52 on, against 0.42 in the changed kernel, and after a stretch with 1.04 us of work from 10 to 13 three of them took 0.64 at 13.64, at a clock of 0.53.
